# The reciprocal roots of the second query sums: the multiplication by the token norms moves from VectorE to GpSimd

## The chip, the cores and the metric

The kernel runs on one core of a Trainium2 chip. The metric is the device time of one execution in microseconds (us); the median over several executions is compared.

## The reference, cut to what matters

One decoder layer for 256 tokens of width 1024: a projection, two groups of attention heads (sparse attention and latent attention), an output projection, and a channel mixer (PEER) that picks 16 of 16384 one-neuron experts per head. The change lies in the mixer. There `h` is normalised with a gain and each token's query of every head is normalised again before it is compared with the keys:

```
q = _rms((xt @ w_q).reshape(T, P_HEADS, P_KEY_DIM)).astype(x.dtype)
s1 = jnp.einsum('thd,hnd->thn', q[..., :half], sub_keys[:, 0]).astype(jnp.float32)
...
vals, ci = lax.top_k(cand, P_TOPK)
g = jax.nn.softmax(vals, axis=-1)
```

`_rms(x)` is `x / sqrt(mean(x*x) + 1e-6)`. A positive factor per token and head doesn't change which keys are the largest, so it is wanted only when the softmax is taken.

## The kernel before, in words

**Stages.** After the attention (to about 165 us) three sets of 512 KB weight tiles are streamed from HBM and counted by one index `s`: 16 of the query projection (`s` 0 to 15), 128 of the experts' input side `u` (16 to 143) and 128 of their output side `v` (144 to 271). The kernel computes all 16384 experts densely and puts the chosen gates on them afterwards.

**What one tile passes through.** `load(s + 5)` sends a DMA from SyncE's queue into one of three `raw` buffers, so the load of tile `s + 5` waits until tile `s + 2` has been read for the last time. `split(s + 3)` makes two operands of it: `hi` is a rounded copy by ScalarE (L798), `lo` is `raw - hi` (L801); that subtraction is the last reader of `raw`. `xproj` (L1135) then runs 24 matmuls on TensorE: for the `u` tiles 16 with `hi`, then 8 with `lo`. `hi` and `lo` have four buffers each.

**Who computes `lo`.** Line 800 chooses while the program is written: in the `u` tiles GpSimd has it while the flag `state["single"]` is set, VectorE otherwise. The flag is set in the two parts of the top-k search that consist of VectorE's MAX8, FIND_INDEX8 and MATCH_REPLACE8 (L1250 to L1255 and L1271 to L1276) and cleared behind them.

**The order of work is fixed.** In this part the schedule is manual: every engine runs its instructions in the order in which the program writes them, and credits (`work_for`) decide while the program is written how many steps of the top-k search stand between two tiles. Nothing is rearranged at run time; an instruction that waits holds up everything behind it on its engine.

**The sums.** `sums()` gives the queries' normalising factors `rq` (128 tokens x 16: 2 token halves x 8 heads). It is a generator with two steps, run while tiles 18 and 20 are handled. The second step (L1407 to L1418) transposes the sums of squares by TensorE, copies them out on VectorE (L1412), multiplies each half by the token's squared norm (L1414, VectorE, a scalar per partition), adds and scales (L149, VectorE), raises to the power -1/2 (L150, GpSimd) and multiplies each half by the token's norm `rs2` (L1416 and L1417). The only reader of `rq` is L1282, behind the candidate search of each half of tokens, ahead of the softmax:

```
V.tensor_tensor(g, vals, vals[:, :, 0:1].broadcast_to((128, 8, 16)), op=ALU.subtract)
V.tensor_tensor(g, g, rq[:, tt * 8:(tt + 1) * 8, None].broadcast_to((128, 8, 16)), op=ALU.mult)
```

On VectorE, L1417 stands between two heads of the first token half's candidate search (L1271 to L1276). Behind that search come L1281 to L1287 and then L801 for tile 26, then L1290 to L1298 and L801 for tiles 27 and 28. On GpSimd, L150 stands between L801 of tile 23 and L801 of tiles 24 and 25.

Of the kernel before, what the change touches and what calls it, by code (L numbers as in the profile page):

```python
# [15 lines left out]
ALU = mybir.AluOpType  # L16
# [69 lines left out]
def body(tc, nc, ap, dbg=None):  # L86
    V, A, T, G, S = nc.vector, nc.scalar, nc.tensor, nc.gpsimd, nc.sync
# [6 lines left out]
    with ExitStack() as ctx:  # L94
# [30 lines left out]
        def bank(name, tag="ps"):  # L125
            return ps.tile([128, 512], F32, tag=tag, name=name, bufs=4 if tag == "ps" else 2)
# [11 lines left out]
        def small(shape, name, dt=F32, bufs=None):  # L138
            return sm.tile(shape, dt, tag=name, name=name, bufs=bufs or 2)
# [6 lines left out]
        def rsqrt(out, ss, n, p=128, m=1):  # L146

            x = small([128, 16], "rs_x")[:p, :m]
            V.tensor_scalar(x, ss, 1.0 / n, EPS, op0=ALU.mult, op1=ALU.add)  # L149
            G.tensor_tensor(out, x, mhalf[:p, :m], op=ALU.pow)  # L150
# [56 lines left out]
        rs2 = misc[:, 118:120]  # L207
# [408 lines left out]

        r_ot = Ring(cm[:, 1024:2048], 512, 2)
        otok, sums, counts = {}, {}, {}

        def unit_B(tt, hp, o):  # L620
# [600 lines left out]
        rq = cst.tile([128, 16], F32, name="rq")  # L1221
# [176 lines left out]
        def sums():  # L1398

            for m in range(8):  # L1400
                p = (m % 4) * 32
                T.matmul(bss[p:p + 1, (m // 4) * 256:(m // 4 + 1) * 256], lhsT=one, rhs=sqq[:, m * 256:(m + 1) * 256], start=True, stop=True)
            qs_ = sqq[:, 1536:2048]
            for p in range(0, 128, 32):
                A.activation(out=qs_[p:p + 1, :], in_=bss[p:p + 1, :], func=AF.Copy)
            yield
            bt = bank("qssT")  # L1407
            for i in range(4):
                T.transpose(bt[:, i * 128:(i + 1) * 128], qs_[:, i * 128:(i + 1) * 128], ident)
            btv = bt.rearrange("p (q t m o) -> p t q m o", q=2, t=2, m=4)[:, :, :, :, 0]  # L1410
            ssq = small([128, 16], "q_ss")
            V.tensor_copy(ssq.rearrange("p (t q m) -> p t q m", t=2, q=2), btv)  # L1412
            for tt in range(2):
                V.tensor_scalar(ssq[:, tt * 8:tt * 8 + 8], ssq[:, tt * 8:tt * 8 + 8], rs2[:, tt:tt + 1], rs2[:, tt:tt + 1], op0=ALU.mult, op1=ALU.mult)  # L1414
            rsqrt(rq, ssq, 256.0, 128, 16)
            for tt in range(2):  # L1416
                V.tensor_scalar(rq[:, tt * 8:tt * 8 + 8], rq[:, tt * 8:tt * 8 + 8], rs2[:, tt:tt + 1], None, op0=ALU.mult)  # L1417
            yield  # L1418
        b = qb
        for s in range(NQ):  # L1420
# [33 lines left out]
        for s in range(NQ, NQ + NU):  # L1454
# [11 lines left out]
            if j == 0:  # L1466
                pend["scores"]()
                qsum = sums()
# [122 lines left out]
```

## Time and profile before

| | us |
|---|---|
| median of 3 executions | 958.29 |
| the three | 958.93, 958.29, 953.25 |
| the profiled execution | 955.38 |
| its span, first to last instruction | 953.6 |
| mean granted TensorE clock, share of full | 0.996 |

The profile is one execution of its own; 1.8 us of its time lie outside the span. In it TensorE is busy 98% of the span, VectorE 75%, ScalarE 53%, GpSimd 16%. PE is TensorE's matmul, PEld its weight load, DVE VectorE, ACT ScalarE, POOL GpSimd, SPq SyncE's DMA queue. Times in rows are us from the start of the span; "xN" means N instructions merged into one row, and a row's length then runs from the first one's start to the last one's end. Brackets at the end of a row give the idle time ahead of it and what ended that.

### The profile page before, as it was taken

Reading aid. Unit: us, or ns where it says so; the run is one execution under the profiler, and the core shown is the slowest. Engines: PE = TensorE matmul, PEld = TensorE weight load, DVE = VectorE, ACT = ScalarE, POOL = GpSimd, SP = SyncE. Lnnn points to the kernel's source line nnn. Section 1 sums busy time; section 2 is a strip of 40 time slices with the busy share of each in tenths; the row PEclk is TensorE's granted clock in tenths of the full one; section 3 lists DMA queues with packets and bytes.
Section 4 is the critical chain, followed back from the end, with each engine's and each line's share of the span. In section 5 each row is a group of like instructions: output and inputs, shape, how many; then the busy total and the mean of one; then the engine's idle time right before and its main releaser. Section 6 shows DMA issues by size and latency. Waiting matters only on the chain.

```text
span 953.6 us, 17117 instructions
## 1 busy us (share of the span) xinstructions
PE 934.6 (98%) x6651; PEld 850.0 (89%) x6651; DVE 712.9 (75%) x1362; ACT 501.0 (53%) x927; POOL 149.5 (16%) x120
## 2 busy tenths in 40 slices
PE   7999999999899999999999999999999999999998
PEld 7887889999899999999999999888888888888886
DVE  6987776858979978889999995566656665566654
ACT  4667765664544465555544444554455445544552
POOL 5331002476038200000111112000000000000000
PEclk9999999999899999999999999999999999999999
DMA  9425214554566665455555555655556565556654
GB/s 333 170 91 176 91 45 156 166 165 135 167 200 187 195 204 170 162 167 166 156 162 170 156 155 194 188 193 197 197 188 192 196 197 191 188 197 198 193 188 151
DMA packets 47313, 166.73 MB, mean 175 GB/s; under 512 B 5504, under 2 KB 6528, under 8 KB 46976
## 3 DMA queue, kind: packets, MB, share of 16 engines
q1 hardware_dynamic: 47232, 165.64, 53.6%
q8 instruction: 52, 0.85, 0.3%
q14 instruction: 29, 0.24, 0.1%
HBM read 163.52 MB, written 2.10 MB: 174 GB/s over the span
## 4 chain that ended last, share of the span: by engine, by line
PE 88%; DVE 8%; ACT 1%; POOL 1%; issue 1%; DMA 0%; SPq 0%; DVEq 0%; POOLq 0%; ACTq 0%
PE y L1508 37%; PE a L1135 35%; PE q L1135 5%; PE g L1351 3%; PE wo L1015 2%; PE oA L708 1%; PE low L314 1%; PE ak L314 1%; PE s L1444 1%; DVE win L281 1%; DVE lo L801 1%; POOL b_rs L150 1%; PE pTA L696 1%; PE sA L677 1%; DVE rq L1417 0%
## 5 line engine op out<-in xcount | busy, mean ns | idle before, releaser
L801 DVE TENSOR_TENSOR lo<-raw,hi 128x1024 fp32r<-128x1024 f32 x236 | 289.1, 1228 | 97.3 <-ACT hi L798 93.3
L798 ACT ACTIVATE hi<-raw 128x1024 fp32r<-128x1024 f32 x266 | 279.8, 1053 | 40.2 <-DMA raw<-u 34.3
L1508 PE MATMUL y<-hi,w 128*128 128x512 f32 x1024 | 274.6, 389 | 0.0
L1135 PE MATMUL a<-xtT,hi 128*128 128x256 f32 x2048 | 262.1, 281 | 0.0
L1135 PEld LDWEIGHTS a<-xtT,hi 128*128 128x128 f32 x2048 | 245.0, 189 | 0.4 <-issue 0.4
L1508 PEld LDWEIGHTS y<-hi,w 128*128 128x128 f32 x1024 | 192.1, 188 | 40.0 <-ACT w L1238 0.3
L1508 PE MATMUL y<-lo,w 128*128 128x512 f32 x512 | 158.4, 389 | 0.0
L1238 ACT ACTIVATE w<-B 128x256 fp32r<-128x256 f32 x128 | 53.4, 417 | 171.2 <-PE y L1508 171.0
L1135 PE MATMUL a<-xtT,lo 128*128 128x256 f32 x1024 | 139.0, 279 | 3.3 <-DVE lo L801 3.3
L1135 PEld LDWEIGHTS a<-xtT,lo 128*128 128x128 f32 x1024 | 127.5, 190 | 3.5 <-DVE lo L801 3.5
L1508 PEld LDWEIGHTS y<-lo,w 128*128 128x128 f32 x512 | 96.1, 188 | 20.0
L1239 DVE TENSOR_TENSOR w<-B,w 128x256 fp32r<-128x256 f32 x128 | 54.4, 426 | 70.1 <-ACT w L1238 70.1
L801 POOL TENSOR_TENSOR lo<-raw,hi 128x1024 fp32r<-128x1024 f32 x30 | 72.2, 2420 | 53.4 <-ACT hi L798 53.1
L1483 POOL TENSOR_TENSOR B<-gl,B 128x512 f32<-128x512 f32 (+33 forms) x37 | 29.7, 802 | 252.2 <-ACT gl L1482 252.2
L1366 ACT ACTIVATE B<-g 128x64 f32<-128x64 f32 (+29 forms) x121 | 23.6, 244 | 76.7 <-DVE B L1364 76.7
L1476 ACT ACTIVATE B<-a 128x512 f32<-128x512 f32 (+33 forms) x59 | 28.1, 477 | 60.7 <-PE a L1135 60.6
L1339 DVE TENSOR_TENSOR oh<-misc,con 128x1024 f16<-128x1024 f16 x64 | 55.9, 874 | 0.0
L1343 DVE TENSOR_TENSOR oh<-oh,gf 128x1024 f16<-128x1024 f16 x64 | 44.3, 692 | 2.2
L1351 PE MATMUL g<-oh 128*128 128x128 f16 x512 | 39.7, 220 | 0.2
L1364 DVE TENSOR_TENSOR B<-g,B 128x8 f32<-128x8 f32 (+32 forms) x69 | 32.7, 479 | 6.2 <-ACT B L1476 6.0
L1135 PE MATMUL q<-xrT,hi 128*128 128x256 f32 x256 | 35.5, 283 | 0.0
L1135 PEld LDWEIGHTS q<-xrT,hi 128*128 128x128 f32 x256 | 32.1, 188 | 0.1
(311 smaller groups left out, 865.8 us busy)
## 6 DMA issues: line engine op xcount, KB each, us to landing
raw<-u SPq DMA_DIRECT2D x128, 512.0 KB, 3.5
raw<-v SPq DMA_DIRECT2D x128, 512.0 KB, 4.3
raw<-wq SPq DMA_DIRECT2D x16, 512.0 KB, 3.4
win<-win SPq DMA_DIRECT2D x10, 512.0 KB, 8.3
w<-w SPq DMA_DIRECT2D x8, 512.0 KB, 3.9
wo<-wout SPq DMA_DIRECT2D x8, 512.0 KB, 6.4
wsm<-wu SPq DMA_DIRECT2D x1, 1280.0 KB, 9.9
xx<-x SPq DMA_DIRECT2D x4, 256.0 KB, 3.3
```

The source lines that it names most:

```text
L798: A.activation(out=hi, in_=src, func=AF.Copy)
L801: e.tensor_tensor(lo, src, hi.bitcast(F32), op=ALU.subtract)
L1135: T.matmul(out, lhsT=w[:, k, :], rhs=xT[:, k, q, :], start=(n == 0 and k == 0), stop=(n == 2 and k == 7))
L1238: A.activation(out=w[:, 0, :], in_=b, func=AF.Copy)
L1239: V.tensor_tensor(w[:, 1, :], b, w[:, 0, :].bitcast(F32), op=ALU.subtract)
L1339: V.tensor_tensor(o[:, 0:2].rearrange("p a t (i two) -> p (a t) i two", two=2), iot.rearrange("p (i two) -> p i two", two=2)[:, None].broa ...
L1343: V.tensor_tensor(pairs(o[:, 2:4]), pairs(o[:, 1:2]).broadcast_to((128, 2, 4, 64, 2)), gf[:, t4, :, :, None, :].broadcast_to((128, 2, 4, 6 ...
L1351: T.matmul(b[:, i, :], lhsT=o[:, 0, i, :], rhs=o[:, 2 + q, i, :], start=(q == 0), stop=(q == 1))
L1364: V.tensor_tensor(w, bv[:, c0:m, :], w, op=ALU.mult)
L1476: A.activation(out=dst[:, :, td:], in_=bv[:, :, td:], func=AF.Gelu_apprx_tanh)
L1483: (G if j < 127 else V).tensor_tensor(dst[:, :, :td], a[:, :, :td], dst[:, :, :td], op=ALU.mult)
L1508: T.matmul(ya[tt][n], lhsT=wh[:, q, tt * 128:(tt + 1) * 128], rhs=src[:, n * 512:(n + 1) * 512], start=(jj == 0 and p == 0), stop=(jj == 1 ...
```

## The change

```
             rsqrt(rq, ssq, 256.0, 128, 16)
             for tt in range(2):
-                V.tensor_scalar(rq[:, tt * 8:tt * 8 + 8], rq[:, tt * 8:tt * 8 + 8], rs2[:, tt:tt + 1], None, op0=ALU.mult)
+                G.tensor_tensor(rq[:, tt * 8:tt * 8 + 8], rq[:, tt * 8:tt * 8 + 8], rs2[:, tt:tt + 1].broadcast_to((128, 8)), op=ALU.mult)
             yield
```

The two multiplications of 128x8 values become GpSimd instructions with two tensor inputs, the second with a step of zero. In GpSimd's order they stand right behind L150, ahead of L801 of tile 24. VectorE's order is the same without the two. All else is unchanged.

## Rows read from the trace of the kernel before

**Rows 1.** The page's part 1: busy us, share of the span, instructions

```profile
PE 934.6 (98%) x6651; PEld 850.0 (89%) x6651; DVE 712.9 (75%) x1362; ACT 501.0 (53%) x927; POOL 149.5 (16%) x120
```

**Rows 2.** TensorE's waits, whole span: total us, times, longest

```profile
PE a L1135 <- DVE lo L801: 3.3, 1, 3.3
PE pTB L646 <- ACT wsm L640: 1.9, 1, 1.9
```

**Rows 3.** The chain that ended last, 205 to 260: start, us, what

```profile
226.51 2.92 POOL rq L150
229.45 4.72 DVE rq L1417 x2
...
241.63 1.23 DVE lo L801
```

**Rows 4.** TensorE's timeline, 223 to 262: tiles 24 to 28

```profile
231.94 2.05 PE L1135 MATMUL a<-xtT,hi 128*128 128x256 f32 x16
233.82 1.11 PE L1135 MATMUL a<-xtT,lo 128*128 128x256 f32 x8
...
236.65 1.11 PE L1135 MATMUL a<-xtT,lo 128*128 128x256 f32 x8
237.59 2.05 PE L1135 MATMUL a<-xtT,hi 128*128 128x256 f32 x16
242.90 2.08 PE L1135 MATMUL a<-xtT,lo 128*128 128x256 f32 x8 [3.26 <-DVE lo L801]
244.78 3.62 PE L1135 MATMUL a<-xtT,hi 128*128 128x256 f32 x16
...
249.50 1.98 PE L1135 MATMUL a<-xtT,hi 128*128 128x256 f32 x16
```

**Rows 5.** Stretches: length, then PE, PEld, DVE, ACT, POOL busy, PEclk, DMA, GB/s

```profile
50.00:100.00 50.00, 46.60 (x386) 39.55 (x387) 39.09 (x93) 34.13 (x91) 11.27 (x8) 1.00 0.40 132
...
242.90:249.50 6.60, 6.60 (x32) 6.60 (x33) 6.46 (x13) 1.06 (x1) 0.00 (x0) 0.54 0.53 176
```

**Rows 6.** Tile rq: duration in ns min/median/max, starts, forms

```profile
L1417 DVE TENSOR_SCALAR rq<-rq,misc x2: 2370/2403/2436, 229.5 to 231.7; 128x8 f32<-128x8 f32 x2
```

**Rows 7.** The timeline of all engines, 215 to 246, VectorE and GpSimd

```profile
215.42 2.64 POOL L801 TENSOR_TENSOR lo<-raw,hi 128x1024 fp32r<-128x1024 f32 x1 [0.46 <-ACT hi L798]
...
221.24 4.75 POOL L801 TENSOR_TENSOR lo<-raw,hi 128x1024 fp32r<-128x1024 f32 x2 [3.17 <-ACT hi L798]
...
221.82 0.24 DVE L1271 MAX8 B<-B 128x8 f32<-128x96 f32 x1
...
229.39 4.75 POOL L801 TENSOR_TENSOR lo<-raw,hi 128x1024 fp32r<-128x1024 f32 x2
...
234.09 0.25 DVE L1271 MAX8 B<-B 128x8 f32<-128x96 f32 x1
...
240.25 0.27 DVE L1281 TENSOR_TENSOR B<-B 128x128 f32<-128x128 f32 x1
```

**Rows 8.** VectorE's timeline, 240 to 300: later subtractions

```profile
245.08 2.36 DVE L801 TENSOR_TENSOR lo<-raw,hi 128x1024 fp32r<-128x1024 f32 x2
...
268.11 1.23 DVE L801 TENSOR_TENSOR lo<-raw,hi 128x1024 fp32r<-128x1024 f32 x1 [1.65 <-ACT hi L798]
```

**Rows 9.** ScalarE's timeline, 195 to 300: rounding tiles 26 and 27

```profile
229.69 1.06 ACT L798 ACTIVATE hi<-raw 128x1024 fp32r<-128x1024 f32 x1 [1.54 <-DMA raw<-u]
...
237.16 1.06 ACT L798 ACTIVATE hi<-raw 128x1024 fp32r<-128x1024 f32 x1 [4.42 <-DMA raw<-u]
```

**Rows 10.** GpSimd's groups by form: busy us, mean ns, idle before

```profile
L150 POOL TENSOR_TENSOR rq<-rs_x,mhalf 128x16 f32<-128x16 f32 x1 | 2.9, 2916 | 0.5 <-PE a L1135 0.5
...
L1483 POOL TENSOR_TENSOR B<-gl,B 128x8 f32<-128x8 f32 x1 | 0.2, 205 | 50.1 <-ACT gl L1482 50.1
```

**Rows 11.** Lines 1414 and 1263: ns min/median/max, starts, forms

```profile
L1414 DVE TENSOR_SCALAR q_ss<-q_ss,misc x2: 278/606/935, 225.1 to 225.9; 128x8 f32<-128x8 f32 x2
...
L1263 DVE TENSOR_TENSOR B<-B x6: 277/480/2465, 215.4 to 306.1; 128x256 f32<-128x256 f32 x2, 128x128 f32<-128x128 f32 x2, 128x384 f32<-128x384 f32 x2
```

More of the change, by code (lines that the diff above doesn't have):

```diff
@@ L1416, in sums @@
             for tt in range(2):
-                V.tensor_scalar(rq[:, tt * 8:tt * 8 + 8], rq[:, tt * 8:tt * 8 + 8], rs2[:, tt:tt + 1], None, op0=ALU.mult)
+                G.tensor_tensor(rq[:, tt * 8:tt * 8 + 8], rq[:, tt * 8:tt * 8 + 8], rs2[:, tt:tt + 1].broadcast_to((128, 8)), op=ALU.mult)
             yield
```

## The prediction

> **What bounds the kernel now.** I read the page first: TensorE is busy for 934.6 of 953.6 us [rows 1], so only what lets TensorE stand still or slows it can move the end. The list of its waits shows where it stands still in the streamed part: once, for 3.3 us, for a `lo` that VectorE was to subtract [rows 2]. The chain of waits shows why that `lo` was late: GpSimd's power, then the two multiplications of L1417 on VectorE, then top-k work, then L801, then TensorE again [rows 3]. TensorE's timeline gives the price. The 16 `hi` matmuls of tile 26 begin at 237.59, its `lo` matmuls only at 242.90 behind 3.26 us of idleness, and tile 27 then takes 4.72 us (244.78 to 249.50), where tiles 24 and 25 together took 5.65 (231.94 to 237.59) [rows 4]. The stretches show what slowed it: from 242.90 to 249.50 the mean granted clock is 0.54, hardly above the lower of its two levels, 1.2 GHz, while TensorE is fully busy [rows 5]. It had been idle just before; the 1.9 us of idleness ahead of L646 [rows 2] lie in an earlier stretch granted 1.00 [rows 5].
>
> So the place costs the wait and a slow stretch behind it. From 237.59 to 249.50 two tiles take 11.91 us; at the pace of the two before they would take 5.65. **The loss at this place is 6.26 us.**
>
> **What the change takes from VectorE.** GpSimd's power begins at 226.51, as soon as VectorE has scaled the sums. VectorE then has nothing to do until 229.45, some 2.9 us, and spends 4.72 us in the two multiplications (2.37 and 2.44 us, for 8 values a partition) [rows 3, 6]; the search goes on at 234.09 [rows 7]. The multiplications run exactly beside two GpSimd subtractions, 4.75 us from 229.39 [rows 7], and each ends when one of those ends; L1414, the same kind of instruction, took 0.28 us at its shortest and 0.94 us when a GpSimd subtraction ran until 225.99 [rows 7, 11]. I read this as VectorE being kept off by GpSimd, not as the price of the multiplication. Without them the search goes on at about 226.5: 7.6 us earlier.
>
> **What comes instead on VectorE.** The candidate search runs 6.16 us (234.09 to 240.25) [rows 7] and doesn't read `rq`, so L1281 is reached at 232.65. Beside GpSimd it ought not to lengthen: the MAX8 of 221.82, beside the subtractions of 221.24 to 225.99, took 0.24 us, that of 234.09, with GpSimd idle, 0.25 [rows 7]. But L1281 takes two tensors, as L1263 does, whose first run beside a GpSimd subtraction took 2.47 us against some 0.28 to 0.5 for such instructions otherwise [rows 7, 11]. GpSimd is then in its last subtraction of the pair (below: until 234.55). I charge the whole of it: L1281 gets through at 234.55, a loss of 1.9 us out of the 7.6. From L1281's start to the end of L801 pass 2.61 us (240.25 to 241.63 + 1.23) [rows 3, 7]; `lo` of tile 26 is ready at 237.2. Its `hi` has been there since 230.75 [rows 9]. TensorE asks for this `lo` at 239.47 (237.59 plus the 1.88 us of 231.94 to 233.82) [rows 4]. **The wait goes, with 2.3 us to spare.**
>
> **What comes on GpSimd.** Two multiplications of 128x8. The trace has no GpSimd multiplication with a step of zero and this length. The nearest row is the 128x8 multiplication of L1483, 205 ns; the far end is the power of 128x16, 2916 ns [rows 10]. I take 0.2 each, 0.41 together, since the kind and size agree and the power is another function. The low end is nothing at all: a gain on GpSimd is excluded, as two instructions are added. Behind them wait `lo` of tiles 24 and 25, ready at 231.77 and 234.14 now (the middle and the end of the 4.75 us from 229.39) [rows 7], needed at 233.82 and 236.65 [rows 4]: 2.05 and 2.51 us to spare, of which 0.41 goes.
>
> The Trainium skill, "GPSIMD Engine Reference" (opening and section 8), speaks against the move: ordinary elementwise work belongs on the Vector engine, about twice as fast. By that rule, as an estimate, the pair would take twice 2 x 0.28, or 1.1 us, still less than the 2.05 to spare, and the sum would stand. The shortest GpSimd row disagrees with it at this size: 205 against 278 ns.
>
> **What is late next.** SyncE's queue and the three `raw` buffers: the load of tile 27 waits for `lo` of tile 24, the load of tile 28 for that of tile 25, so both land 0.41 us later. `hi` of tile 27 is then ready at 237.16 + 1.06 + 0.41 = 238.6 [rows 9]; TensorE wants it at 240.42, 1.8 us later. VectorE comes to `lo` of tile 27 at 237.2 + 2.2 (242.86 to 245.08) [rows 3, 8] = 239.4 and has it by 240.6; wanted at 242.3. The load of tile 29 waited for `lo` of tile 26 and so goes out 5.7 us earlier, beside those two: it may slow them, which is what the 1.8 us are for. Reading `rq` in L1282 costs no wait: it is ready by 229.9, L1282 comes after 234.
>
> **Later.** Without the gap TensorE is 6.26 us further on, VectorE 5.7. By 268.11 VectorE itself waits for ScalarE's `hi` ahead of a subtraction [rows 8] while TensorE never idles, so the suppliers have caught up there, and what follows starts from full buffers as before.
>
> **The sum.** 955.38 of the profiled execution less 6.26 is 949.1. That execution lies 2.9 under the median of 958.29 and 2.1 over the lowest of the three; the same gain from the median gives 952.0. I put the forecast between the two: 950.5.
>
> **Rivals.**
>
> *The gap is moved, not removed.* The new wait is for `hi` or `lo` of tile 27: three loads in flight together, or VectorE held up longer by GpSimd than charged. For it: the margins are 1.8 us. Against it: each margin was worked out with the full charge. With an unchanged `lo` order a remaining gap of 1 to 2 us, as short as the one ahead of L646 that kept its clock, costs itself alone: gain 4 to 5, time 950.4 to 954.
>
> *The slow stretch is worth more in other executions.* The executions at 958 are some 3 us longer than the profiled one. If their slow stretch here lasts twice as long, another 6.6 us at half the clock costs 3.3 us more, and the change takes back 9.5 of 958.3: 948.8, 1.0% faster. For it: the spread needs a cause. Against: nothing in the trace says that it lies here.
>
> *Dear GpSimd multiplications: the other side.* If the small multiplication with a step of zero costs as much as the power, 2.92 each, `lo` of tile 24 is 5.83 late against 2.05 to spare, and TensorE stands still for 3.8 us at tile 24. That is longer than the 3.26 that stood before a slow stretch; with one like it (6.26 - 3.26 = 3.0) the loss is 6.8 where 6.26 is won: 955.9, slower than before by half a microsecond. It decides from about 2.65 us each (2 x 2.65 - 2.05 = 3.25); under 1.02 each nothing waits. Against it stands the 205 ns row. Together with some further delay through late loads it may pass 1%.
>
> *The change doesn't give what it says.* The gap goes, but the lead is lost again later, where top-k of the second half and the one-hots load VectorE: 955.4. Against it: TensorE's only wait on `lo` in the whole span is this one [rows 2].
>
> **How the numbers follow.** Forecast 0.68 (own range 947 to 954, the runs' spread of 2 to 3 us around 950.5); gap moved 0.10; worth more 0.14; dear multiplications 0.04, half of it past 1%; lead lost again 0.04. The range 946 to 956 leaves out the tail of the second rival, most of the last two and the tips of the spread. About 1% is what a measurement of this kernel can tell from no change. 6.26 us are 0.65%, so the forecast lies within 1%. Faster by over 1%: the second rival and the tips of the forecast, 0.17. Slower by over 1%: 0.03. Within: 0.80.
>
> **What would show it.** Right: no wait of TensorE on L801 near 240; a granted clock of 1.00 from 220 to 268; two GpSimd multiplications of about 0.2 us at 229.4; VectorE's search going on at 226.5; L1281 lengthened to about 2 us beside GpSimd; tiles 26 and 27 at 2.8 us each. Wrong: GpSimd rows of 1 us or more there, a wait of TensorE for `hi` or `lo` of tiles 24 to 28, a clock that falls elsewhere after 250, or `rq` read late at L1282.

## The result, and the profile after

| | before | after |
|---|---|---|
| median of 9 executions, us | 956.92 | 951.83 |
| lowest to highest, us | 953.25 to 961.58 | 948.76 to 953.64 |
| the profiled execution, us | 955.38 | 953.64 |
| its span, us | 953.6 | 951.9 |

The ratio after to before is 0.9939, 95% interval 0.9918 to 0.9959: 4 to 8 us are won, 5.8 by the middle of it; the two medians lie 5.1 apart. The forecast was 950.5 us and a change within 1%: the measured 951.83 lies 1.3 us over it, inside the range of 946 to 956, and the change is within 1%. One execution among those of the experiments below, of the late kernel's second measurement, took 1159.69 us at a mean granted clock of 0.754 and is left out of its row. The profiled execution after is the longest of its nine, so the two spans differ by 1.7 us only; where the rest of that went comes below.

First TensorE's timeline after, tiles 24 to 29 (start, length, engine, line; columns as in [rows 4]):

```profile
236.89 2.05 PE L1135 MATMUL a<-xtT,hi 128*128 128x256 f32 x16
238.77 1.11 PE L1135 MATMUL a<-xtT,lo 128*128 128x256 f32 x8
...
242.54 2.05 PE L1135 MATMUL a<-xtT,hi 128*128 128x256 f32 x16
244.42 1.11 PE L1135 MATMUL a<-xtT,lo 128*128 128x256 f32 x8
245.37 2.05 PE L1135 MATMUL a<-xtT,hi 128*128 128x256 f32 x16
247.25 1.11 PE L1135 MATMUL a<-xtT,lo 128*128 128x256 f32 x8
248.19 2.05 PE L1135 MATMUL a<-xtT,hi 128*128 128x256 f32 x16
```

Tile 24 begins at 236.89 here and at 231.94 in [rows 4]: this execution comes 4.95 us later into the place, which the change can't reach. All times after are read against that shift. Tile 26 begins at 242.54, exactly 4.95 later than before, tile 28 at 248.19 instead of 249.50: between them 5.65 us instead of 11.91. **The 6.26 us are gone to the hundredth.** The stretch is granted the full clock; its row (length, then busy time of the five engines, PEclk, DMA share, GB/s) answers to [rows 5]:

```profile
238.00:260.00 22.00, 22.00 (x189) 22.00 (x189) 21.43 (x33) 12.72 (x15) 1.53 (x1) 1.00 0.69 215
```

Next the timeline of VectorE, GpSimd and ScalarE after, the lines that answer to [rows 7] to [rows 9]:

```profile
231.20 0.17 DVE L149 TENSOR_SCALAR rs_x<-q_ss 128x16 f32<-128x16 f32 x1
231.28 0.25 DVE L1271 MAX8 B<-B 128x8 f32<-128x96 f32 x1
231.46 2.91 POOL L150 TENSOR_TENSOR rq<-rs_x,mhalf 128x16 f32<-128x16 f32 x1 [0.51 <-DVE rs_x L149]
...
234.45 0.36 POOL L1417 TENSOR_TENSOR rq<-rq,misc 128x8 f32<-128x8 f32 x2
...
234.77 4.76 POOL L801 TENSOR_TENSOR lo<-raw,hi 128x1024 fp32r<-128x1024 f32 x2
...
237.46 2.22 DVE L1281 TENSOR_TENSOR B<-B 128x128 f32<-128x128 f32 x1
240.86 1.22 DVE L801 TENSOR_TENSOR lo<-raw,hi 128x1024 fp32r<-128x1024 f32 x1
242.27 1.06 ACT L798 ACTIVATE hi<-raw 128x1024 fp32r<-128x1024 f32 x1 [4.59 <-DMA raw<-u]
...
244.32 2.35 DVE L801 TENSOR_TENSOR lo<-raw,hi 128x1024 fp32r<-128x1024 f32 x2
```

The search goes on right behind L149; the two GpSimd multiplications take 0.36 us together; L1281, the first VectorE instruction with two tensors beside GpSimd, takes 2.22 us instead of the 0.27 of [rows 7]; `lo` of tile 26 is ready at 242.08 and wanted at 244.42.

**Where 4.6 us of the 6.26 went in the two profiles.** The spans differ by 1.7 us only. In the attention stage the granted clock fell three times after and not once before. The same three stretches, after, then before:

```profile
15.00:25.00 10.00, 9.20 (x63) 8.92 (x64) 5.54 (x13) 3.19 (x8) 5.61 (x5) 0.83 1.01 408
60.00:75.00 15.00, 13.07 (x95) 12.33 (x93) 11.03 (x29) 7.53 (x28) 4.17 (x3) 0.89 0.23 70
130.00:140.00 10.00, 8.93 (x45) 6.47 (x43) 6.07 (x17) 6.30 (x24) 0.55 (x1) 0.83 0.18 55
```

```profile
15.00:25.00 10.00, 9.35 (x79) 9.08 (x80) 6.70 (x15) 3.82 (x10) 5.56 (x5) 1.00 1.02 411
60.00:75.00 15.00, 13.07 (x103) 12.02 (x102) 10.90 (x28) 10.16 (x36) 2.61 (x2) 1.00 0.22 70
130.00:140.00 10.00, 10.00 (x75) 8.83 (x75) 6.88 (x18) 7.50 (x25) 0.00 (x0) 1.00 0.17 53
```

All of this lies ahead of the change, and the programs are the same there. The fall in the second of these stretches stands behind TensorE's wait of 1.93 us ahead of L646. All fourteen profiles (before, after and the twelve runs below) have this wait, of 1.85 to 1.94 us. In eight of them the clock fell within 1.4 us of its end, in the other six, the kernel before among them, it didn't. Here is the stretch behind the wait in the profile of the change run once more (experiment 1), then in that of the kernel before:

```profile
62.60:66.40 3.80, 3.77 (x20) 3.63 (x20) 2.27 (x7) 3.31 (x16) 2.06 (x1) 0.55 0.50 167
```

```profile
62.40:66.20 3.80, 3.80 (x33) 3.55 (x34) 2.27 (x8) 3.80 (x18) 2.06 (x1) 1.00 0.47 154
```

So the same short wait can be followed by a fallen clock in one execution and not in the next. The stream of tiles starts 4.95 us later (159.72 against 154.77). So the profiles are compared from the start of the stream on: +4.95 ahead of it, -6.26 from tile 26 to 28, and then this, TensorE at tile 37 and its neighbours before and after:

```profile
271.51 2.07 PE L1135 MATMUL a<-xtT,hi 128*128 128x256 f32 x16
...
274.33 1.98 PE L1135 MATMUL a<-xtT,hi 128*128 128x256 f32 x16
```

```profile
271.06 2.08 PE L1135 MATMUL a<-xtT,hi 128*128 128x256 f32 x16
...
273.87 1.98 PE L1135 MATMUL a<-xtT,hi 128*128 128x256 f32 x16
```

At tile 37 the lead is 0.46 us (274.33 - 273.87); at tile 28 it was 1.31. **0.85 us were given back**: behind the gap the kernel before ran tiles of 2.72 us, while after the change the 2.83 us of the tiles ahead simply went on to tile 35 (experiment 5 returns to the two paces). The remaining 1.2 us of the spans' difference come later; nearly all of it is the last ten tiles of `u`, which ran at 2.83 us before and at 2.72 after.

### The profile page after: what moved, and what is told of

Its sections match the earlier page's. It is cut to its first block, busy times and chain, and to the rows that moved or that the text cites. A ratio compares the mean times of both kernels' runs of the same rounds, so it can differ in the third digit from the quotient of the medians.

```text
span 951.9 us, 17118 instructions
## 1 busy us (share of the span) xinstructions
PE 934.8 (98%) x6651; PEld 850.1 (89%) x6651; DVE 710.0 (75%) x1360; ACT 501.0 (53%) x927; POOL 150.1 (16%) x122
## 4 chain that ended last, share of the span: by engine, by line
PE 90%; DVE 6%; ACT 1%; issue 1%; POOL 1%; DMA 0%; SPq 0%; DVEq 0%; ACTq 0%
PE y L1508 37%; PE a L1135 36%; PE q L1135 5%; PE g L1351 3%; PE wo L1015 2%; PE oA L708 1%; PE low L314 1%; PE ak L314 1%; PE s L1444 1%; DVE win L281 1%; POOL b_rs L150 1%; PE pTA L696 1%; PE sA L677 1%; DVE lo L801 1%; PE tx L296 0%
## 5 line engine op out<-in xcount | busy, mean ns | idle before, releaser
L801 DVE TENSOR_TENSOR lo<-raw,hi 128x1024 fp32r<-128x1024 f32 x236 | 289.3, 1228 | 96.8 <-ACT hi L798 93.1
L801 POOL TENSOR_TENSOR lo<-raw,hi 128x1024 fp32r<-128x1024 f32 x30 | 72.3, 2422 | 47.5 <-ACT hi L798 47.3
```

The source lines that it names most:

```text
L801: e.tensor_tensor(lo, src, hi.bitcast(F32), op=ALU.subtract)
```

## The experiments

Ratios are to the kernel before, run beside each on the same chip.

| kernel | median us (runs) | ratio, 95% interval | wait of TensorE on `lo`, us |
|---|---|---|---|
| the change | 951.83 (9) | 0.9939, 0.9918 to 0.9959 | none |
| the change again | 950.43 (8) | 0.9933, 0.9907 to 0.9958 | none |
| late on VectorE | 949.09 (4) | 0.9930, 0.9914 to 0.9947 | none |
| late on VectorE again | 952.02 (11) | 0.9954, 0.9932 to 0.9975 | none |
| one VectorE instruction | 952.93 (7) | 0.9968, 0.9956 to 0.9979 | 1.7 |
| one more power on GpSimd | 951.21 (7) | 0.9954, 0.9938 to 0.9970 | 1.6 |
| two more powers on GpSimd | 956.44 (10) | 1.0009, 0.9992 to 1.0026 | 4.3 |

**1. Is it the engine or the place?** The multiplications stay on VectorE, behind the search:

```
 # sums(): the two lines of L1416 and L1417 are left out
 # topk_steps(tt), ahead of L1281:
+            if tt == 0:
+                for half in range(2):
+                    V.tensor_scalar(rq[:, half * 8:half * 8 + 8], rq[:, half * 8:half * 8 + 8], rs2[:, half:half + 1], None, op0=ALU.mult)
```

> The two multiplications stay on VectorE, with a scalar per partition, but stand behind the first half's candidate search, right ahead of L1281. Theory 'the place' (VectorE waited there for the power and then for GpSimd's subtractions; which engine multiplies matters little): the search goes on right behind L149, the first multiplication is held until GpSimd's subtraction of tile 25 ends, the second takes some 0.3 us, the subtraction of tile 26 ends 2 us or more before TensorE wants it, no idleness of TensorE there, ratio to before 0.993 to 0.996, as with the change. Theory 'the engine' (two multiplications on VectorE cost 2.4 us each by themselves): 4.7 us stand ahead of the subtraction of tile 26 again, of which the 2.3 to spare hide half: TensorE idle for 2 us or more, ratio 0.996 to 1.000.

Measured: 0.9930, and no wait. VectorE's timeline in this kernel (L1282 is the moved pair, L1284 the old L1281), with GpSimd's two subtractions and the two durations of the tile `rq`:

```profile
226.49 0.17 DVE L149 TENSOR_SCALAR rs_x<-q_ss 128x16 f32<-128x16 f32 x1
...
229.64 4.75 POOL L801 TENSOR_TENSOR lo<-raw,hi 128x1024 fp32r<-128x1024 f32 x2
...
232.74 1.80 DVE L1282 TENSOR_SCALAR rq<-rq,misc 128x8 f32<-128x8 f32 x2
234.46 0.28 DVE L1284 TENSOR_TENSOR B<-B 128x128 f32<-128x128 f32 x1
...
235.85 1.22 DVE L801 TENSOR_TENSOR lo<-raw,hi 128x1024 fp32r<-128x1024 f32 x1
```

```profile
L1282 DVE TENSOR_SCALAR rq<-rq,misc x2: 217/944/1672, 232.7 to 234.3; 128x8 f32<-128x8 f32 x2
```

The same two instructions that took 4.72 us [rows 3] take 1.80 here: the first is held for 1.67 us until the second of GpSimd's two subtractions ends (at 234.39 in this profile), the second takes 0.22. L1284 behind them then takes its 0.28. So the gain is that of the place: nothing on VectorE has to wait for the power, and only one instruction meets GpSimd's subtraction. That GpSimd multiplies isn't needed for it. Run once more beside the change:

> The multiplications on VectorE behind the first half's search once more. Theory 'the place decides, not the engine': the same as the change within 0.2%. Other theory 'late on VectorE is the better place' (its first measurement was 0.9930, the change's 0.9939): lower than the change beyond the intervals. Between those two I expect no difference.

> The change itself once more, beside the other three on the same chip. Expected: no wait of TensorE in the streamed part, tile 26 and 27 at 2.72 or 2.83 us, ratio to before 0.992 to 0.996. Where the attention stage starts the streamed part earlier than 159 us (eight profiles so far: 154.5 to 159.5), the profiled execution is as much shorter.

Measured: 0.9954 and 0.9933. The same late kernel gave 0.9930 the first time; the intervals overlap in all directions, and no difference from the change is shown.

**2. Half of the hold-up.** One instruction in the old place instead of two:

```
-            for tt in range(2):
-                V.tensor_scalar(rq[:, tt * 8:tt * 8 + 8], rq[:, tt * 8:tt * 8 + 8], rs2[:, tt:tt + 1], None, op0=ALU.mult)
+            r3 = rq.rearrange("p (t m) -> p t m", t=2)
+            V.tensor_tensor(r3, r3, rs2[:, :, None].broadcast_to((128, 2, 8)), op=ALU.mult)
```

> One VectorE instruction of 128x16 with two tensor inputs in the old place, instead of two of 128x8. Theory 'held up per instruction': it waits for the power as before, is held by one GpSimd subtraction, 2.3 to 2.5 us instead of 4.7; the subtraction of tile 26 ends 2.4 us earlier than before, TensorE idle for 0.8 to 1.2 us instead of 3.3, granted clock stays full, ratio 0.994 to 0.997. Theory 'priced by the work': 4.7 us for the same 16 values, nothing gained, ratio 1.000.

The tile `rq` in this kernel, then TensorE's timeline:

```profile
L1417 DVE TENSOR_TENSOR rq<-rq,misc x1: 2366/2366/2366, 231.3 to 231.3; 128x16 f32<-128x16 f32 x1
```

```profile
242.43 1.19 PE L1135 MATMUL a<-xtT,lo 128*128 128x256 f32 x8 [0.93 <-DVE lo L801]
...
245.88 1.19 PE L1135 MATMUL a<-xtT,lo 128*128 128x256 f32 x8 [0.45 <-DVE lo L801]
```

The 16 values cost 2.37 us in one instruction and 4.72 in two: the price goes by the GpSimd subtraction that each instruction meets, not by the values. The wait at tile 26 is as expected; a second one at tile 27 was not: VectorE comes to that `lo` 2.2 us behind the first and has no slack left. The table's 1.7 us hold a third wait, of 0.30 us at tile 56, far behind the place; its cause is not shown. From tile 26 to 28 the loss is 1.80 us instead of 6.26. The clock was granted in full (1.00 from 238 to 250).

**3. Reading the scalar.** The old kernel with a constant in place of the norm:

```
-                V.tensor_scalar(rq[:, tt * 8:tt * 8 + 8], rq[:, tt * 8:tt * 8 + 8], rs2[:, tt:tt + 1], None, op0=ALU.mult)
+                V.tensor_scalar(rq[:, tt * 8:tt * 8 + 8], rq[:, tt * 8:tt * 8 + 8], 1.5, None, op0=ALU.mult)
```

> The kernel before with the two VectorE multiplications by a constant 1.5 instead of a scalar per partition read from memory (the token norms are left out of the factor). Theory 'held up by GpSimd': each still takes some 2.4 us beside a GpSimd subtraction, TensorE's wait on tile 26 and the slow stretch stay. Theory 'reading the scalar per partition is what waits': 0.1 to 0.3 us each, the subtraction of tile 26 is 4 us earlier, no wait of TensorE there.

One execution took 956.96 us, beside one of the kernel before at 960.28. The tile `rq`, then TensorE's waits on `lo` (total us, times, longest):

```profile
L1417 DVE TENSOR_SCALAR rq<-rq x2: 158/1264/2369, 231.1 to 233.3; 128x8 f32<-128x8 f32 x2
```

```profile
PE a L1135 <- DVE lo L801: 2.0, 2, 1.6
```

Neither theory has it whole. The first is held for a whole GpSimd subtraction without any scalar to read, so reading it isn't what waits. The second ran in 0.16 us just as GpSimd went from one subtraction to the next; with the scalar per partition the second was held too [rows 6]. TensorE still waited, 1.58 and 0.45 us, at tiles 26 and 27. Why the form with the constant slips in and the other doesn't stays open.

**4. The rival made real: GpSimd as dear as the power.** The change with one, then two more powers behind the multiplications, results unused:

```
+            for k in range(1):   # 2 in the second kernel
+                G.tensor_tensor(small([128, 16], "spare"), rq, mhalf, op=ALU.pow)
```

> The change, with one more power of 128x16 (2.9 us, result unused) on GpSimd behind the two multiplications. Theory 'margin of 2.05 us ahead of tile 24's subtraction': 0.4 and 2.9 less 2.05 make TensorE idle for 1.2 to 1.4 us at tile 24, and nowhere else; the clock holds, ratio to before 0.995 to 0.997. Theory 'the margin is smaller or the late loads come on top': 2 us or more of idleness, at tiles 24 to 28, perhaps a fallen clock, ratio 0.998 to 1.002.

> The change, with two more powers of 128x16 (5.8 us, results unused) on GpSimd behind the two multiplications: the rival of dear GpSimd multiplications made real. Theory: TensorE idle for 4.1 to 4.3 us at tile 24, behind it a stretch at half the clock that costs about 3 us, as before at tile 26: ratio to before 1.000 to 1.002, TensorE's wait on the subtraction moved from tile 26 to tile 24. Other theory 'the clock fell before for another reason than the idleness': 4.2 us of idleness alone, ratio 0.997 to 0.998.

TensorE's timeline with one, then with two, and the stretch behind the second's wait:

```profile
235.86 1.19 PE L1135 MATMUL a<-xtT,lo 128*128 128x256 f32 x8 [1.60 <-POOL lo L801]
```

```profile
238.26 2.08 PE L1135 MATMUL a<-xtT,lo 128*128 128x256 f32 x8 [4.27 <-POOL lo L801]
```

```profile
238.00:244.00 6.00, 5.74 (x27) 5.74 (x28) 4.41 (x8) 1.06 (x1) 2.59 (x2) 0.51 0.65 214
```

With one, 1.60 us of idleness where 1.2 to 1.4 were expected, one wait only, at tile 24, and the clock holds (1.00 from 232 to 250). With two, 4.27 us, the clock falls to its lower level, and the ratio is 1.0009: the whole gain is eaten, as the rival had it, within 0.2%. The wait with one power is 0.2 to 0.4 us over the expected one, that with two inside it, so the margin ahead of tile 24 is about what the rows said; both kernels ran tiles 22 and 23 at 2.72 us and not 2.83, which alone brings TensorE to tile 24 0.2 us earlier. In the streamed part of these profiles the clock goes with the length of the wait: at 3.26 [rows 4] and 4.27 us it fell, at 1.60, 1.58 and 0.93 it held. That is no dividing line: behind the 1.9 us ahead of L646 it fell in eight profiles of fourteen.

The second kernel also shows what it is on GpSimd that holds VectorE:

```profile
230.13 5.78 POOL L1419 TENSOR_TENSOR spare<-rq,mhalf 128x16 f32<-128x16 f32 x2
...
233.07 0.30 DVE L1282 TENSOR_TENSOR B<-B,rq 128x128 f32<-128x128 f32 x1
...
234.16 1.22 DVE L801 TENSOR_TENSOR lo<-raw,hi 128x1024 fp32r<-128x1024 f32 x1
...
235.87 4.72 POOL L801 TENSOR_TENSOR lo<-raw,hi 128x1024 fp32r<-128x1024 f32 x2
235.94 2.42 DVE L1293 CAST B<-B 128x256 f16<-128x256 f32 x1
```

Beside the two powers, L1282 and L801 with two tensors each take their usual 0.30 and 1.22 us; beside the subtraction a cast with one tensor takes 2.42 instead of its usual 0.29. It is the subtraction that holds VectorE here, not a busy GpSimd as such.

**5. The pace of 2.83 or 2.72 us a tile.** The fourth transpose of the sums (L1409) is done twice, in the change and in the late version, and three times in the change:

```
-            for i in range(4):
+            for i in (0, 1, 2, 3, 3):   # (0, 1, 2, 3, 3, 3) for six
                 T.transpose(bt[:, i * 128:(i + 1) * 128], qs_[:, i * 128:(i + 1) * 128], ident)
```

> The change with the fourth transpose of the sums (L1409) done twice. With the change, tiles 21 to 35 take 2.83 us each, where tiles 37 to 64 take 2.72; with the kernel before, tiles 28 to 35 took 2.72, behind the gap. Theory 'TensorE falls into one of two paces, set by what interrupted the stream last': with one more short matmul in the interruption tiles 22 to 35 may take 2.72, some 1.4 us less in all. Theory 'the stretch is slow for another reason (GpSimd, loads, VectorE at work beside it)': 2.83 again. In both, nothing else moves by more than 0.2 us.

> The change with the fourth transpose of the sums done twice, once more. Theory 'the extra transpose sets the pace': tiles 22 to 35 at 2.72 us again, ratio 0.001 to 0.002 below the change's. Theory 'it differs from one execution to the next' (three other kernels had 2.72 us there without it, four had 2.83): either pace, the same ratio.

> Both in one kernel: the multiplications on VectorE behind the first half's search, and the fourth transpose of the sums done twice. Theory 'the extra transpose sets the pace': tiles 22 to 35 at 2.72 us in the profile, ratio to before some 0.0014 below that of the late multiplications alone. Theory 'the pace after the sums differs from one execution to the next': the pace may be either, the ratio the same as without it.

> The change with five transposes, a fourth look (five transposes so far: 2.72 us a tile behind the sums in three profiles of three; four transposes: 2.72 in four, 2.83 in five). Theory 'five transposes set the pace': 2.72 again. Theory 'chance': either.

> The change with the fourth transpose done three times, six in all. Theory 'the length of the interruption decides the pace': another pace than with five is possible, 2.83 us a tile. Theory 'anything longer than four frees the stream' : 2.72. Theory 'chance': either; then this look and the other say no more than one more throw each.

Three of these kernels were executed once each, beside one execution of the kernel before: 953.48 us beside 960.28 (the change with five, the first time), 950.55 beside 956.06 (the change with five, the third time) and 949.80 beside 956.06 (six).

Tiles of the change with five transposes (the third time; the other three profiles with five show the same pace), then two tiles of the change again, with four:

```profile
237.61 1.98 PE L1135 MATMUL a<-xtT,hi 128*128 128x256 f32 x16
239.43 1.07 PE L1135 MATMUL a<-xtT,lo 128*128 128x256 f32 x8
240.33 1.98 PE L1135 MATMUL a<-xtT,hi 128*128 128x256 f32 x16
```

```profile
227.68 1.98 PE L1135 MATMUL a<-xtT,hi 128*128 128x256 f32 x16
...
230.40 1.98 PE L1135 MATMUL a<-xtT,hi 128*128 128x256 f32 x16
```

With five, tiles 22 and on take 2.72 us in four profiles of four; with six, 2.83 in one; with four, 2.83 in five profiles (the change's among them) and 2.72 in four (the change again among them). The ratios with five are 0.9925 (0.9899 to 0.9952) in the change and 0.9923 (0.9893 to 0.9954) in the late version, against 0.9933 for the change and 0.9954 for the late version beside them; the intervals overlap. A gain of 1.4 us is in the profiles' tiles, not in the ratios. If the number of transposes had nothing to do with the pace, the four profiles with five would all fall among the eight quick ones of these thirteen about once in ten times (an estimate from the counts): **that five sets the pace is suggested, not shown, and no version beyond the change is shown to be faster than it.**

## Why the prediction was right, point by point

Times of the profile after have the 4.95 us taken off.

- **The price of the place**, 6.26 us: tiles 26 and 27 take 5.65 instead of 11.91. Right. That the slow stretch is the idleness's doing was inferred then and is borne out by experiment 4: with the idleness moved to tile 24 the slow stretch moved with it. It is a price of these executions, not of every one (below).
- **What held VectorE** was GpSimd and not the work: experiments 1 and 2 show it, 1.80 and 2.37 us for what took 4.72. Experiment 4 narrows it to the subtraction.
- **L1281 held up instead**: forecast until 234.55, measured until 234.73 (237.46 + 2.22 - 4.95). `lo` of tile 26: forecast 237.2, measured 237.13; wanted 239.47 in both.
- **GpSimd's multiplications**: 0.41 forecast, 0.36 measured for the pair, 202 ns each. The step of zero costs nothing that can be seen. The prediction set 205 against VectorE's 278 ns, a multiplication by two scalars; the same multiplication on VectorE, not held up, took 217 (experiment 1).
- **Next in line**: `hi` of tile 27 forecast 238.6, measured 238.38; its `lo` forecast 240.6, measured 240.54 (the middle of the 2.35 us from 244.32), wanted at 242.3. The three loads at once didn't slow each other by as much as the margin.
- **Later**: no wait of TensorE in the streamed part. But "what follows starts from full buffers as before" left out the pace: behind the gap the kernel before ran eight tiles at 2.72 us, the change at 2.83, and 0.85 us were given back. Between these two profiles the place is thus worth 5.4 us. It is no fixed term of the sum, for the change again ran the same tiles at 2.72 (experiment 5); whether the ratio's 5.8 us lie under 6.26 for this reason is not shown.
- **"As short as the one ahead of L646 that kept its clock"**: in the rival of the moved gap a wait of 1 to 2 us costs itself alone. That was read from one profile; behind that very wait the clock fell in eight of the fourteen. The rival didn't come about, so the forecast didn't rest on it.
- **The rival "worth more in other executions"**: no slow stretch other than those behind a wait is seen in the streamed part of any profile. The stream starts anywhere from 154.8 to 159.7 us, and the fallen clock of the attention stage goes with it: not once in the profiles that start at 154.8, 155.3 and 155.5, three times in the two that start at 159.7. By the recorded clock the slow stretch of the kernel before is worth less in some executions: of the 43 beside the experiments, seven have a mean clock of 0.998 or 1.000, where 6.6 us at 0.54 alone would leave 0.997. Their median is 954.71 us, that of the other 36 is 956.08. Times of 952.87 to 957.44 among the seven show that the clock doesn't account for the whole spread; what else does stays open.
- **The median**: the forecast lay between 949.1 and 952.0; nine executions gave 951.83, and the three of before at 958.29 stood 1.4 us over the nine.

## What to carry to other kernels

Where a tiny instruction takes microseconds, look at what the other engines do beside it, and then move it to where nobody is waiting behind it; which engine it goes to matters less. A wait of a few microseconds on a full TensorE is to be priced with the clock behind it: in the profiles here 1.6 us of idleness cost 1.9 (a tile of 4.60 instead of 2.72), and 3.3 us cost 6.3. One profile doesn't settle that price, so read the same wait in several. Before two profiles are set against each other, line them up at the start of the stage in question.

## What the runs showed that was not expected

- TensorE runs the same 24 matmuls at one of two steady paces, 2.72 or 2.83 us (113 or 118 ns a matmul), at the full granted clock and with no wait; it changes from one to the other only at short interruptions of the stream (transposes, a wait).
- A VectorE multiplication by a constant, 8 values a partition, took 2.37 us and its neighbour 0.16: beside a busy GpSimd the price of an instruction depends on the moment that it comes.
- GpSimd's power takes 2.91 us for 16 values a partition, its multiplication 0.20 for 8. In experiment 4 the power held nothing on VectorE for all that time, where a subtraction of 2.4 us does.
